# Routing of a two-layer diffusion block: unscaled router weights against modulated tokens, the norm's shift on VectorE, an earlier table load

## The chip, the cores and the metric

The kernel runs on one core of a Trainium2 chip. The metric is the device time of one execution in microseconds: the median of three runs of the kernel before is 1811.23 us (1810.03 to 1813.2).

## The reference

Two layers work on 256 latent tokens and 256 context tokens, each of width 1024. A layer normalises and modulates its tokens, mixes them (windowed attention with a sink beside a bidirectional gated recurrence), adds and normalises, and then sends them through 16 experts, each of which picks its own 32 tokens of a stream:

```python
mod = jax.nn.silu(c) @ w_mod[l] + b_mod[l]                 # 6 x 1024 columns, for both streams
u = layer_norm(x) * (1.0 + sc1) + sh1
y, yc = token_mixer(u, uc, w_in[l], ...)
x = post_norm(ALPHA * x + g1 * y, ln_g[l, 0], ln_b[l, 0])
u = layer_norm(x) * (1.0 + sc2) + sh2
x = post_norm(ALPHA * x + g2 * expert_choice_ffn(u, w_router[l], w_gate[l], w_up[l], w_down[l]), ...)

def expert_choice_ffn(u, w_router, w_gate, w_up, w_down):
    aff = softmax(u @ w_router)                            # (256, 16), float32
    top_w, top_idx = top_k(swapaxes(aff, 1, 2), 32)        # each expert picks 32 tokens
    h = silu(xs @ w_gate) * (xs @ w_up)                    # xs: the picked rows of u
    y = (h @ w_down) * top_w, added back to its tokens
```

In layer 0 both streams go through all of it; in layer 1 only the latent stream does.

## The kernel before, in words

Tokens stand in four tiles of 128 rows (`X[t]`), two for each stream; layer 1 has two. Everything is in one program whose instructions are put in a static order for each engine: a list scheduler takes the program's operations with their data dependences and with the tile buffers that they share, plays them against a model of durations, and writes down in which order each engine takes them. Some chains are fixed by `in_order`, and routing has a higher priority. At run time each engine takes its instructions strictly in that order, so an instruction that waits holds up all behind it. A DMA that GpSimd issues stands in GpSimd's order too.

The work runs through these stages. **Start** (to about 57 us): `crow` (the two conditioning vectors), the small parameter rows `rows` and the modulation biases `brow` are loaded into rotating 512-column buffers (`t2`, two of them), transposed by TensorE (L186, L205, L235/L236) and copied to columns. `mod_first` (L257 on) streams the modulation weights `wmod`, multiplies them by the conditioning columns `scol` in four groups (L267), turns the row by a transposition (L272) and adds the bias columns `bmod` (L276); the result `modT` is what every modulated token needs. ScalarE rounds the first input weights `win` to `wh` (L478), and VectorE and GpSimd each take half of the difference `wl` (L479); the projections (L168 to L170) are three matmuls for each product.

**Mixers**, then **post-norm**, then **routing** (`route`, one call for each stream): `ln_plain` normalises a token tile into `xh`. With `act` it is done on ScalarE as `r*x + (-mu*r)`; the column `mr` = -mu*r is made by two GpSimd multiplies (L343, L344), after the inverse root, which is a power on GpSimd (L333). TensorE transposes `xh` in two halves of 512 columns (L1061), which are copied to `u` (L1063, one by ScalarE and one by VectorE); the router weights, loaded to `wraw` (L1034) and scaled by the modulation on GpSimd (L1040), stand still and `u` moves past them in 128 columns (L1065). That leaves four partial sums on four bands of partitions; L1044/L1045 make the part of the shift, L1068 adds it, and L1070 folds the four bands and transposes to tokens x experts. Then softmax (L1072 to L1075, the exponential on ScalarE), the transposition to experts x tokens (L1077), four rounds of an eight-fold maximum (L1082/L1083), a scan that ranks the picked tokens (L1086 to L1088), and a one-hot matrix (L1102). **Experts**: the one-hot matrix gathers tokens by matmul (L1136), `modulate` writes them to `xs` (L383 on VectorE, L385 on ScalarE), and gate, up and down matmuls (L1218, L1251) run as their weights arrive. SyncE issues all weight loads in order; each waits until a buffer is free. At the very end `finish_out` (L1293 on) normalises the output, one half of a token tile on ScalarE and GpSimd, three on VectorE.

## Time and profile before

| | us |
|---|---|
| median of three runs | 1811.23 |
| profiled execution | 1812.94 |
| its span | 1811.2 |
| start, to the first steady projections | 0 to 57 |
| mixers of layer 0 | 57 to 500 |
| post-norm and routing of layer 0 | 500 to 535 |
| experts of layer 0 | 535 to 982 |
| mixers of layer 1 | 982 to 1325 |
| post-norm and routing of layer 1 | 1325 to 1356 |
| experts of layer 1, and the end | 1356 to 1811 |

TensorE is busy 1562.6 us (86%), VectorE 677.1 (37%), ScalarE 450.0 (25%), GpSimd 305.1 (17%); the DMA engines move 526 MB. By the page's chain of work that ended last, 53% of the span is TensorE's and 37% DMA's. How to read it: the shares are means over stages with different limits, so what an edit is worth is read in its own stage, from which wait ends last there. In a row of the timeline stand the start, the duration, the engine (PE is TensorE, DVE VectorE, ACT ScalarE, POOL GpSimd, SP SyncE), the line, the operation, the tile written and the tiles read, the shape, and in brackets how long the engine had been idle and what released it.

### The profile page before, as it was taken

What the parts mean: (1) busy time and instruction counts of PE and PEld (TensorE: products, weight loads), DVE (VectorE), ACT (ScalarE), POOL (GpSimd) and SP (SyncE); (2) the same over time, 40 slices, a digit from 0 to 9 for tenths busy, and PEclk for the clock granted to TensorE, in tenths of its full rate; (3) what the DMA queues carried; (4) which work ended last, traced back from release to release, by engine and by line L of the source; (5) the groups of instructions that cost most, each with busy time, mean ns of one, the idle gap of its engine ahead of it and who ended that gap; (6) DMA issues with size and microseconds to landing.
All of it is one profiled execution on the core that took longest, in us unless ns stands there. A gap on an engine that the chain in (4) does not pass through costs nothing.

```text
span 1811.2 us, 27388 instructions
## 1 busy us (share of the span) xinstructions
PE 1562.6 (86%) x11342; PEld 925.0 (51%) x11342; DVE 677.1 (37%) x1430; ACT 450.0 (25%) x850; POOL 305.1 (17%) x302
## 2 busy tenths in 40 slices
PE   6999999999989999997998899998968766666666
PEld 4777776688754433332323788775845222322222
DVE  4546566323661221211213756666751100100102
ACT  2436556323120100101000533576410000000000
POOL 2342121123310000000002633331610000000001
PEclk9999999999979999999999999999979777867887
DMA  9644123533679999999999653424689999999997
GB/s 323 186 117 127 60 82 129 177 126 117 245 308 385 421 421 421 421 422 421 421 421 379 208 178 105 130 92 131 241 341 408 421 421 422 420 421 421 421 421 287
DMA packets 159436, 526.06 MB, mean 290 GB/s; under 512 B 9896, under 2 KB 94064, under 8 KB 111184
## 3 DMA queue, kind: packets, MB, share of 16 engines
q1 hardware_dynamic: 157136, 517.46, 74.1%
q0 software_dynamic: 1456, 4.49, 0.7%
q10 hardware_dynamic: 720, 2.36, 0.4%
q8 instruction: 89, 1.46, 0.3%
q14 instruction: 35, 0.29, 0.0%
HBM read 523.23 MB, written 1.05 MB: 289 GB/s over the span
## 4 chain that ended last, share of the span: by engine, by line
PE 53%; DMA 37%; DVE 4%; ACT 2%; POOL 2%; issue 1%; SPq 1%; POOLq 0%; ACTq 0%; DVEq 0%
DMA w<-in_w_up_dram 13%; DMA w<-in_w_down_dram 12%; PE acc L168 9%; DMA w<-in_w_gate_dram 9%; PE acc L170 8%; PE acc L169 8%; PE acc L1218 8%; PE o L1251 4%; DMA wmod<-in_w_mod_dram 3%; PE md L294 2%; PE sc L701 2%; PE sc L724 1%; PE o L663 1%; PE tr L719 1%; PE hs L649 1%
## 5 line engine op out<-in xcount | busy, mean ns | idle before, releaser
L1218 PE MATMUL acc<-w,xs 128*32 128x256 f32 (+1 forms) x3064 | 402.9, 512 | 92.0 <-DMA w<-in_w_up_dram 48.9
L1218 PEld LDWEIGHTS acc<-w,xs 128*32 128x32 f32 (+1 forms) x3064 | 138.0, 130 | 339.2 <-issue 175.9
L1251 PE MATMUL o<-w,hT 128*32 128x256 f32 (+1 forms) x1432 | 188.9, 507 | 44.9 <-DMA w<-in_w_down_dram 30.5
L168 PE MATMUL acc<-uTh,wh 128*128 128x512 f32 (+1 forms) x592 | 215.1, 365 | 3.0 <-ACT qr L682 1.3
L169 PE MATMUL acc<-uTl,wh 128*128 128x512 f32 (+1 forms) x592 | 212.0, 358 | 1.4 <-DVE uTl L398 1.4
L170 PE MATMUL acc<-uTh,wl 128*128 128x512 f32 (+1 forms) x592 | 210.1, 355 | 0.0
L1229 ACT ACTIVATE h<-acc 128x512 f32<-128x512 f32 (+1 forms) x32 | 15.7, 491 | 522.2 <-PE acc L1218 509.4
L479 POOL TENSOR_TENSOR wl<-win,wh 128x1024 fp32r<-128x1024 f32 x44 | 113.4, 2579 | 164.3 <-ACT wh L478 164.3
L1251 PEld LDWEIGHTS o<-w,hT 128*32 128x32 f32 (+1 forms) x1432 | 63.5, 130 | 149.0 <-issue 66.7
L1230 DVE TENSOR_TENSOR h<-h,acc 128x512 f32<-128x512 f32 (+1 forms) x32 | 17.7, 552 | 293.4 <-PE acc L1218 293.4
L168 PEld LDWEIGHTS acc<-uTh,wh 128*128 128x128 f32 x592 | 111.9, 190 | 28.0 <-issue 6.7
L169 PEld LDWEIGHTS acc<-uTl,wh 128*128 128x128 f32 x592 | 112.3, 190 | 18.3 <-issue 2.8
L170 PEld LDWEIGHTS acc<-uTh,wl 128*128 128x128 f32 x592 | 112.1, 189 | 17.6 <-issue 3.4
L478 ACT CAST wh<-win 128x1024 fp32r<-128x1024 f32 x84 | 84.0, 1047 | 88.0 <-PE acc L169 61.9
L1110 POOL TENSOR_TENSOR OW<-OH,aff 128x256 f32<-128x256 f32 x8 | 4.9, 616 | 583.9 <-PE sc L1233 569.0
L1274 DVE TENSOR_TENSOR Y<-o,g2 OH 32x512 f32<-32x512 f32 x60 | 41.2, 687 | 140.1 <-PE o L1251 139.3
L479 DVE TENSOR_TENSOR wl<-win,wh 128x1024 fp32r<-128x1024 f32 x40 | 51.7, 1294 | 84.8 <-ACT wh L478 84.6
L1235 ACT COPY hT<-sc 128x512 f32<-128x512 f32 (+1 forms) x32 | 15.3, 479 | 243.1 <-PE sc L1233 243.1
L1274 DVE TENSOR_TENSOR Y g<-o,Y g 32x256 f32<-32x256 f32 x60 | 25.2, 420 | 122.0 <-PE o L1251 121.3
L294 PE MATMUL md<-wmod,scol 128*32 128x256 f32 x640 | 59.0, 416 | 7.8 <-DMA wmod<-in_w_mod_dram 5.6
L564 DVE TENSOR_TENSOR K<-K,F 128x512 f32<-128x512 f32 x56 | 46.6, 832 | 8.9 <-PE hs L630 5.4
L333 POOL TENSOR_TENSOR mv<-mv,nhalf 128x1 f32<-128x1 f32 x26 | 24.4, 942 | 126.7 <-DVE mv L332 126.0
(450 smaller groups left out, 2373.3 us busy)
## 6 DMA issues: line engine op xcount, KB each, us to landing
w<-in_w_gate_dram SPq DMA_DIRECT2D x128, 1024.0 KB, 19.8
w<-in_w_up_dram SPq DMA_DIRECT2D x127, 1024.0 KB, 19.8
w<-in_w_down_dram SPq DMA_DIRECT2D x119, 1024.0 KB, 19.8
wmod<-in_w_mod_dram SPq DMA_DIRECT2D x80, 512.0 KB, 4.6
win<-in_w_in_dram SPq DMA_DIRECT2D x26, 1024.0 KB, 5.4
win<-in_w_in_dram SPq DMA_DIRECT2D x32, 512.0 KB, 5.3
wmod<-in_w_mod_dram SPq DMA_DIRECT2D x32, 256.0 KB, 5.9
wo<-in_w_out_dram SPq DMA_DIRECT2D x8, 1024.0 KB, 5.0
```

Of the source, the lines that this page charges most:

```text
L168: mm(p, a.hi, b.hi, start=start, stop=False, **kw)
L169: mm(p, a.hi, b.lo, start=False, stop=False, **kw)
L170: mm(p, a.lo, b.hi, start=False, stop=stop, **kw)
L294: mm(pm[32 * j:32 * j + 32, 0:256], scol[:, k, :], w[:, 256 * j:256 * j + 256], start=(k == 0), stop=(k == KT - 1))
L333: pows.append(nc.gpsimd.tensor_tensor(mv[:, 2:3], mv[:, 2:3], nhalf[:, 0:1], op=ALU.pow))
L478: nc.scalar.copy(hi[:, r], w[:, r])
L479: ins = eng.tensor_sub(lo[:, r], w[:, r], hi[:, r])
L564: nc.vector.tensor_tensor(kv, kv, _view(f, 0, [[nf + 1, 2], [2, nf // 2], [0, m]]), op=ALU.mult)
L701: mm(p[:, :nk], qT[:, hd // 2, tk], kT[:, 2 * g + par, k0:k0 + nk], start=True, stop=True)
L1218: ins = mm(p[MW * j:MW * j + MW, :NW], xs[:, k, e4, :], wrow(w, k)[:, NW * j:NW * j + NW], start=(k == 0), stop=(k == KT - 1))
L1251: mm(py[MW * dj:MW * dj + MW, :NW], hT[:, 128 * m + MW * j:128 * m + MW * j + MW], wrow(wd, kt)[:, NW * dj:NW * dj + NW], start=(kt == 0), ...
L1274: nc.vector.tensor_tensor(o, py[r:r + 32, :NW], g2[r:r + 32, NW * dj:NW * dj + NW], op=ALU.mult)
```

## The change

- `wrt`, a permanent tile, takes the router weights unscaled. `router_load` issues its two loads of 32 KB on GpSimd's queue, for layer 0 among the mixers' first steps in the program text and for layer 1 after layer 0's first gather. The scaling, the memory fill, the bias matmuls, the shift's copy and the folding matmul go.
- In `route` the transposed tokens are modulated by scale and shift in four pieces of 128x128 for each half; for the last stream ScalarE and VectorE take the pieces in turn, before that ScalarE takes all. A piece stands still and 16 columns of router weights move past it; eight such matmuls for a token tile add up in PSUM, in a fixed order.
- `mr` is made by one VectorE instruction in `ln_plain` and in `finish_out`.
- `warm`, an exponential of one column, stands after the branches of the mixers.
- `sg` and `lt`, so far permanent tiles, come from the rotating pair `t2`.
- Two constant blocks of the table `cst` go.

```diff
-C_ID, C_ROT, C_COS, C_SIN, C_WM, C_TRI, C_ONE, C_IOTA, C_SEL, C_SUM, C_END = (
-    0, 128, 256, 512, 768, 1024, 1152, 1280, 1312, 1408, 1424)
+C_ID, C_ROT, C_COS, C_SIN, C_WM, C_IOTA, C_SEL, C_SUM, C_END = (
+    0, 128, 256, 512, 768, 1024, 1056, 1152, 1168)
...
+    wrt = P.tile([128, KT, NE], F32, name="wrt")
+
+    def router_load(l):
+        for i in range(2):
+            nc.gpsimd.dma_start(wrt[:, i::2], _dram(w_router, l * D * NE + i * NE, [[2 * NE, 128], [256 * NE, KT // 2], [1, NE]]))
...
-    sg = P.tile([128, 16], F32, name="sg")
+    sg = t2("sg")[:, :16]
...
-    lt = P.tile([128, 4, 2, HH], F32, name="lt")
+    lt = t2("lt")[:, :32].rearrange("p (a d h) -> p a d h", a=4, d=2)
...
-            nc.gpsimd.tensor_tensor(m, mu, r, op=ALU.mult)
-            pows.append(nc.gpsimd.tensor_tensor(m, m, neg, op=ALU.mult))
+            nc.vector.tensor_scalar(m, mu, -1.0, r, op0=ALU.mult, op1=ALU.mult)
...
             chains()
+            router_load(l)
...
+        warm = T.tile([128, 1], F32, name="warm", tag="warm", bufs=1)
+        nc.scalar.activation(warm, sgs[1, KT - 1][:, 0:1], AF.Exp)
...
-        wr = M["oT"].rearrange("p s (k e) -> p s k e", k=KT)
-        wraw = t2("wraw")[:, :KT * 32].rearrange("p (k e) -> p k e", e=32)
-        nc.gpsimd.memset(wraw, 0.0)
-        for i in range(2):
-            nc.gpsimd.dma_start(wraw[:, i::2, 0:NE], _dram(w_router, l * D * NE + i * NE, [[2 * NE, 128], [256 * NE, KT // 2], [1, NE]]))
-
-        pl = tr()
-        bcol = T.tile([128, 2], F32, name="bcol", tag="bcol")
-        for s in range(S):
-            for h in range(2):
-                nc.gpsimd.tensor_tensor(wr[:, s, 4 * h:4 * h + 4], wraw[:, 4 * h:4 * h + 4],
-                                        MT[l][:, 8 + h, :, s, None].to_broadcast([128, 4, 32]), op=ALU.mult)
-            for k in range(KT):
-                j = k % 4
-                mm(pl[32 * j:32 * j + 32, s:s + 1], wraw[:, k], MT[l][:, 6 + k // 4, j, s:s + 1], start=(k == j), stop=(k > j))
-        nc.vector.tensor_copy(bcol[:, 0:S], pl[:, 0:S])
...
+            busy = s == S - 1
+            turns = []
...
+                o = pl[:, NE * i:NE * i + NE]
                 for h in range(2):
...
-                    (nc.vector.tensor_copy if h else nc.scalar.copy)(u, p)
                     for m in range(4):
-                        mm(pl[32 * m:32 * m + 32, 128 * i:128 * i + 128], wr[:, s, 4 * h + m], u[:, 128 * m:128 * m + 128],
-                           start=(h == 0), stop=(h == 1))
-                lT = tp("lT")[:, :128]
-                nc.vector.tensor_scalar(lT, pl[:, 128 * i:128 * i + 128], bcol[:, s:s + 1], None, op0=ALU.add)
-                o = pl[:, 256 + NE * i:256 + NE * i + NE]
-                mm(o, lT, cst[:, C_SUM:C_SUM + NE], start=True, stop=True)
+                        um, k = slice(128 * m, 128 * m + 128), 4 * h + m
+                        modulate(busy and m % 2, u[:, um], p[:, um], l, 3, 4, k, s)
+                        in_order(turns, mm(o, u[:, um], wrt[:, k], start=(k == 0), stop=(k == KT - 1), skip_group_check=True))
...
+        if not last:
+            router_load(l + 1)
...
-            nc.gpsimd.tensor_tensor(m, *sc[0], op=ALU.mult)
-            nc.gpsimd.tensor_tensor(m, m, neg, op=ALU.mult)
             seq = []
+            in_order(seq, nc.vector.tensor_scalar(m, sc[0][0], -1.0, sc[0][1], op0=ALU.mult, op1=ALU.mult))
```

The static order changes with it, also where the text does not. GpSimd at the start, before (`brow` the modulation biases, `wl` the difference halves of the first input weights):

```order
L198 DMA msk<-in_msk_dram 128x192
L200 DMA sink<-in_attn_sink_dram 128x16
L203 DMA rows<-in_hgrn_lb_fw_dram 8x128
L203 DMA rows<-in_hgrn_lb_bw_dram 8x128
L203 DMA rows<-in_hgrn_norm_g_dram 8x128
L333 ISA
L333 TENSOR_TENSOR mv<-mv,nhalf 128x1
L232 DMA brow<-in_b_mod_dram 48x256
L333 TENSOR_TENSOR mv<-mv,nhalf 128x1 x3
L479 TENSOR_TENSOR wl<-win,wh 128x1024 x2
```

The same engine and place after the change, in the new file's line numbers (L235 is the load of `brow`, L481 the difference, L186 the router weights):

```order
L201 DMA msk<-in_msk_dram 128x192
L203 DMA sink<-in_attn_sink_dram 128x16
L186 DMA wrt<-in_w_router_dram 128x4x16 x2
L336 ISA
L336 TENSOR_TENSOR mv<-mv,nhalf 128x1
L206 DMA rows<-in_hgrn_lb_fw_dram 8x128
L206 DMA rows<-in_hgrn_lb_bw_dram 8x128
L206 DMA rows<-in_hgrn_norm_g_dram 8x128
L336 TENSOR_TENSOR mv<-mv,nhalf 128x1 x3
L481 TENSOR_TENSOR wl<-win,wh 128x1024 x2
L235 DMA brow<-in_b_mod_dram 48x256
```

The load of `brow` has moved behind three powers and two differences, the loads of `rows` behind the first power, and the router loads stand ahead of it all.

TensorE at the start, before, from the transpositions of `brow` on (`xh` normalised tokens, `md` the modulation row, `uTh`/`uTl` modulated tokens; a count is of issued instructions, where the trace counts two for each of these float32 matmuls):

```order
L235 MATMUL o<-cst,brow 128x48
L236 MATMUL o<-cst,brow 128x48
L235 MATMUL o<-cst,brow 128x48
L236 MATMUL o<-cst,brow 128x48
L272 MATMUL md<-cst,row 128x128
L376 MATMUL o<-cst,xh_149 128x128 x4
L376 MATMUL sc<-cst,xh_149 128x128 x8
L267 MATMUL md<-wmod,scol 32x128 x16
L168 MATMUL acc<-uTh,wh 128x512 x2
```

The same engine and place after (L238/L239 the transpositions of `brow`, L270 the modulation matmuls, L378 the tokens' transpositions, L166 to L168 the projections):

```order
L208 MATMUL o<-cst,rows 128x24
L275 MATMUL md<-cst,row 128x128
L238 MATMUL o<-cst,brow 128x48
L239 MATMUL o<-cst,brow 128x48
L238 MATMUL o<-cst,brow 128x48
L239 MATMUL o<-cst,brow 128x48
L378 MATMUL o<-cst,xh_148 128x128 x4
L270 MATMUL md<-wmod,scol 32x128 x32
L378 MATMUL sc<-cst,xh_148 128x128 x4
L166 MATMUL acc<-uTh,wh 128x512
L167 MATMUL acc<-uTl,wh 128x512
```

Behind `brow` now stand all 32 modulation matmuls of the second group ahead of the first projection, where 16 stood before.

VectorE in layer 1's routing, after, from the normalisation of the second token tile's post-norm to the logits (`X_3197` that token tile, `u_10108` and the like the modulated pieces, `r_10131` the first maximum of the softmax):

```order
L372 SCALAR_TENSOR_TENSOR X_3197<-X_3197,mv,lnp 128x1024
L326 BN_STATS st<-X_3197 128x6
L385 TENSOR_SCALAR u_10108<-sc,modT_108 128x128
L326 BN_STATS st<-X_3197 128x6
L385 TENSOR_SCALAR u_10122<-sc,modT_108 128x128
L385 TENSOR_SCALAR u_10108<-sc,modT_108 128x128
L332 BN_AGGR mv<-st 128x2
L335 TENSOR_SCALAR mv<-mv 128x1
L385 TENSOR_SCALAR u_10122<-sc,modT_108 128x128
L349 TENSOR_SCALAR xh<-X_3197,mv 128x1024
L1062 TENSOR_REDUCE r_10131<-tr 128x1
```

Before, the two statistics stood side by side there, and one copy of 128x512 stood between the statistics and the normalisation of the second token tile; now four pieces stand among them.

## Rows read from the trace of the kernel before

**Rows 1.** By stage, layer 0: us, busy by engine, clock, DMA share, GB/s.

```profile
57.00:500.00 443.00, 436.00 (x2925) 324.28 (x2924) 234.21 (x495) 197.33 (x376) 129.09 (x110) 0.99 0.41 136
...
500.00:535.00 35.00, 27.66 (x242) 20.77 (x242) 27.29 (x87) 9.27 (x21) 4.50 (x9) 0.71 0.78 323
```

**Rows 2.** GpSimd's timeline at the start: start, duration, instruction, idle before.

```profile
6.80 0.60 POOL L232 DMA_DIRECT2D brow<-in_b_mod_dram  x1
...
26.66 2.44 POOL L479 TENSOR_TENSOR wl<-win,wh 128x1024 fp32r<-128x1024 f32 x1 [1.17 <-ACT wh L478]
```

**Rows 3.** Landing of the DMAs of the tile brow.

```profile
DMA to landing us min/median/max: 6.1/6.1/6.1
```

**Rows 4.** Landing of the DMAs of the tile rows.

```profile
DMA to landing us min/median/max: 7.4/7.5/7.5
```

**Rows 5.** Two stretches of the start, columns as in group 1.

```profile
6.00:8.00 2.00, 0.25 (x1) 0.17 (x1) 2.00 (x5) 0.56 (x2) 1.13 (x2) 1.00 1.14 197
...
28.00:30.00 2.00, 2.00 (x16) 1.11 (x8) 2.00 (x2) 0.00 (x0) 1.10 (x1) 0.69 1.10 355
```

**Rows 6.** TensorE's timeline at the start.

```profile
18.06 0.26 PE L235 MATMUL o<-cst,brow 48*128 48x48 f32 x1
...
25.96 2.67 PE L267 MATMUL md<-wmod,scol 128*32 128x128 f32 x32
...
39.60 0.71 PE L168 MATMUL acc<-uTh,wh 128*128 128x512 f32 x2
...
45.38 1.95 PE L267 MATMUL md<-wmod,scol 128*32 128x128 f32 x64
...
47.27 0.66 PE L376 MATMUL sc<-cst,xh 128*128 128x128 f32 x4
...
47.68 0.70 PE L168 MATMUL acc<-uTh,wh 128*128 128x512 f32 x2
```

**Rows 7.** VectorE's timeline at the start.

```profile
19.65 0.23 DVE L276 TENSOR_TENSOR modT<-md,bmod 128x4 f32<-128x4 f32 x2
...
25.67 1.23 DVE L479 TENSOR_TENSOR wl<-win,wh 128x1024 fp32r<-128x1024 f32 x1 [1.20 <-ACT wh L478]
```

**Rows 8.** Two stretches ahead of expert weights, columns as in group 1.

```profile
530.00:535.00 5.00, 4.39 (x35) 4.04 (x36) 2.07 (x6) 2.00 (x5) 0.00 (x0) 1.00 0.00 0
...
1354.00:1356.00 2.00, 2.00 (x22) 1.88 (x24) 0.82 (x2) 0.92 (x2) 0.00 (x0) 1.00 0.00 0
```

**Rows 9.** VectorE in layer 0's routing.

```profile
515.03 0.69 DVE L1063 COPY u<-sc 128x512 f32<-128x512 f32 x1 [0.87 <-PE sc L1061]
...
517.40 0.35 DVE L1068 TENSOR_SCALAR lT<-hs,bcol 128x128 f32<-128x128 f32 x1
...
529.42 0.41 DVE L383 TENSOR_SCALAR xs<-o,modT 128x128 f32<-128x128 f32 x1 [0.53 <-ACT xs L385]
```

**Rows 10.** TensorE in layer 0's routing.

```profile
517.81 0.61 PE L1070 MATMUL hs<-cst,lT 128*128 128x16 f32 x2 [0.16 <-DVE lT L1068]
```

**Rows 11.** GpSimd in layer 1's routing.

```profile
1328.66 1.90 POOL L333 TENSOR_TENSOR mv<-mv,nhalf 128x1 f32<-128x1 f32 x2 [4.63 <-DVE mv L332]
...
1330.81 1.13 POOL L344 TENSOR_TENSOR mr<-mr,neg 128x1 f32<-128x1 f32 x1
```

**Rows 12.** ScalarE in layer 1's routing.

```profile
1331.97 1.24 ACT L345 ACTIVATE xh<-X,mr,mv 128x1024 f32<-128x1024 f32 x1 [23.84 <-POOL mr L344]
...
1338.63 1.28 ACT L1073 ACT_TABLE_LOAD   x1
```

**Rows 13.** GpSimd at the front of layer 1.

```profile
1000.66 0.28 POOL L344 TENSOR_TENSOR mr<-mr,neg 128x1 f32<-128x1 f32 x1
```

**Rows 14.** GpSimd at the end.

```profile
1802.02 0.55 POOL L333 TENSOR_TENSOR mv<-mv,nhalf 128x1 f32<-128x1 f32 x1 [65.03 <-DVE mv L332]
...
1806.25 1.59 POOL L1307 TENSOR_TENSOR X<-X,lnp 128x512 f32<-128x512 f32 x1
```

**Rows 15.** ScalarE at the end.

```profile
1804.05 0.78 ACT L1305 ACTIVATE X<-hs,mr,mv 128x512 f32<-128x512 f32 x1 [16.41 <-POOL mr L1298]
```

More of the change, by code (lines that the diff above doesn't have):

```diff
@@ L68, in _shape_tables @@
     cst[:, C_WM + 128:C_WM + 256] = np.where(j >= p, 0.0, NEG)
-    cst[:, C_TRI:C_TRI + 128] = (p < j)
-    cst[:, C_ONE:C_ONE + 128] = 1.0
     cst[:, C_IOTA:C_IOTA + 32] = np.arange(1, 33)[None, :]
@@ L182, in tile_kernel @@
     nc.gpsimd.memset(nhalf, -0.5)
-    neg = P.tile([128, 1], F32, name="neg")
-    nc.gpsimd.memset(neg, -1.0)
+    wrt = P.tile([128, KT, NE], F32, name="wrt")
+    def router_load(l):
+        for i in range(2):
+            nc.gpsimd.dma_start(wrt[:, i::2], _dram(w_router, l * D * NE + i * NE, [[2 * NE, 128], [256 * NE, KT // 2], [1, NE]]))
     pt = tr()
```

## The prediction

> **What bounds the kernel now.** I read the views in this order: the stage table, the start's timelines, the DMA landings, the rows around the two routings, the tail. In the stage table the reader sees that layer 0's mixers are TensorE's: 436.0 of 443 us busy, DMA at 0.41, and in the routing stage behind them it is still 27.66 of 35 [rows 1]. Behind routing the kernel waits for expert weights, but these cannot run ahead: just before the first gate matmuls the DMA share is 0.00 in layer 0 and again in layer 1 [rows 8], because the weight buffers are full until the experts start. So whatever is gained or lost ahead of a first expert matmul, at the start of the kernel too, goes on to the end. That makes the first 57 us, where TensorE waits for modulation, as important as the two routings.
>
> **The start: the bias load moves behind GpSimd's casts.** Before, GpSimd issues the DMA of `brow` (all modulation biases) at 6.80, and it lands 6.1 us later, long before TensorE transposes it at 18.06 [rows 2, 3, 6]. The change takes `sg` and `lt` out of the permanent pool into the two rotating buffers of `crow`, `rows` and `brow`; a static order is planned with that, and in it the issue of `brow` stands behind both weight subtractions of GpSimd, the second of which starts at 26.66 and takes 2.44 [rows 2]. These wait for ScalarE's casts, and those for the first weights, none of which the change makes earlier. So the issue comes at 26.66 + 2.44 = 29.10.
>
> Landing: the row for this very DMA is 6.1, and for the three small ones of `rows` it is 7.4 to 7.5 [rows 3, 4]. Both ran while the DMA engines were full (share 1.14 in 6 to 8), and at 28 to 30 the share is 1.10 [rows 5], so I take 6.1: the transposes begin at 35.2 and not at 18.06. The ends are 0 us (then 29.7, the issue alone) and 7.5 (36.6). The two router loads of 32 KB that now ride in the full stream at the very beginning I book at nothing; their cost, if any, lies inside that upper end. VectorE's two subtractions also stand ahead of its small work now, but the later one ends at 25.67 + 1.23 = 26.90 [rows 7], with eight microseconds to spare.
>
> The Trainium skill gives another price here ("DMA: Bandwidth & Descriptors", section "Anatomy of one DMA — SWDGE (gpsimd) path"): about 2.0 us fixed plus the bytes over 436 GB/s, an estimate of 2.1 for 48 KB. The transposes would then begin at 31.2. The trace does not agree in a full stretch: 6.1 and 7.4 [rows 3, 4], and the measurement decides.
>
> Behind the waiting transposes, on TensorE's own queue, stand the modulation matmuls of the second group and every projection matmul, so the engine stands still. From the start of the transposes to the end of the first modulation columns it took 19.65 + 0.23 - 18.06 = 1.82 [rows 6, 7]; that gives 37.0. Then come 64 modulation matmuls, which cost 1.95 at the full clock and 2 x 2.67 = 5.34 at the rate seen after TensorE's pause before 25.96, where the stage's clock was low [rows 6]. After an even longer pause I take 4.4: 41.4. Four transposes (0.66) bring the first projection to 42.1. One group's period before was 47.68 - 39.60 = 8.08; in the new order each carries four transposes more, so about 8.7. Two periods: 59.5 for the point that stood at 47.68. By then TensorE has done the same matmuls in both kernels. **Delay: 59.5 - 47.68 = 11.8 us.** With a landing of 3 us it is 8.7; at the outer ends (at once, full clock; 7.5, half clock) 3.9 and 14.1. The mixers behind keep their order on TensorE and VectorE, and TensorE has 7.0 us idle in 443 there, each bit waiting for work that moves along [rows 1]. So nothing takes the delay in.
>
> **Routing, layer 0: +1.0.** Away goes, for the last token tile, the copy with the bias (0.35) and the folding matmul (0.61) [rows 9, 10]: -0.96. One copy of 128x512 (0.69) becomes four modulations of 128x128, alternating between ScalarE and VectorE on one PSUM bank. How that runs is to be seen at `xs`, the same kind of alternation: each VectorE piece waits 0.53 for ScalarE's [rows 9]. So the two engines don't overlap on one bank, and four hand-overs cost 4 x 0.53 - 0.69 = +1.43. In the gather the two banks change places in ScalarE's order, and the first gate matmul waits one hand-over more: +0.53. Sum +1.0. Ends: -1.0 if the pieces overlap, +2.5 if the second half pays as well. Router scaling and the bias matmuls leave GpSimd and TensorE; they lie beside the post-norm, so I book nothing. The exponential's table load moves among the mixers, where ScalarE is busy 197 of 443 [rows 1]: nothing either.
>
> **Front of layer 1: -0.3.** One of two GpSimd multiplies ahead of the normalisation goes (0.28) [rows 13]. Ends -1.5 and +0.5.
>
> **Routing, layer 1: -1.3.** The normalisation starts at 1331.97, right behind the negation (1330.81 + 1.13), which stood behind two powers (1328.66, 1.90) [rows 11, 12]. With the shift on VectorE behind the first power (half of 1.90, so 1329.6) it could start 2.1 earlier. But that is the first token tile; the second is normalised by VectorE, which now has quarter copies and a wait for GpSimd ahead of it. I count 0.5 of the 2.1. The table load of 1.28 at 1338.63 lies between two logit copies and the exponential, on the path: -1.28 [rows 12]. Links -0.96 and quarters +1.43 as in layer 0. Sum -1.3; ends -4.3 (everything counts, no price for the quarters) and 0.
>
> **Tail: -0.8.** The power ends at 1802.57, but ScalarE's half starts only at 1804.05, behind a second power and the negation; GpSimd's last add, at 1806.25 for 1.59, follows from it [rows 14, 15]. At most 1.25 is to be had; VectorE, which now waits for that power too, gives some back. Ends -1.25 and 0.
>
> **Sum.** 11.8 + 1.0 - 0.3 - 1.3 - 0.8 = +10.4 on the profiled execution's 1812.94 (span 1811.2). That execution is 1.7 above the median of 1811.23, so I put the difference on the median: **1821.6**.
>
> **Rivals.**
> - *The biases land quickly*, in about 3 us. For it: 48 KB is little. Against it: all four rows of that queue in a full stretch. Delay 8.7, time 1818.5. The page's price named above would mean 7.8 and 1817.6.
> - *The last stream's routing becomes the longer one.* VectorE now waits for GpSimd's power and takes pieces in turn with ScalarE, and its reductions queue behind those pieces; both routings at their upper ends are +2.8 more: 1824.5. For it: the 0.53 waits. Against it: the pieces for the first tokens lie beside other work.
> - *The routing gains in full*: the first tile's 2.1 us carries through, and the quarters cost nothing: layer 0 at -1.0, layer 1 at -4.3, so 11.8 - 1.0 - 0.3 - 4.3 - 0.8 = +5.4, 1816.6.
> - *Not slower: the late start is swallowed.* Place: between the first projections and layer 0's first gate matmul. If something other than TensorE set the end of the mixers, a start up to 11.8 us late would cost nothing, and the rest gives 1.0 - 0.3 - 1.3 - 0.8 = -1.4: 1809.8. It decides from the point where TensorE has more than about 8 us to spare in layer 0's mixers; it has 7.0, in pieces that themselves hang on its own chain [rows 1]. For it speaks only that matmul ends are modelled, so a busy engine may hide slack.
>
> **How the numbers follow.** A difference under 0.2% (3.6 us) can't be told from none here. Chances: forecast 0.66 (its own range 1818 to 1825.5), quick landing 0.14, longer routing 0.07, full gain 0.05, swallowed 0.08. The first four are slower, but for some 0.04 where short landing and good routing meet: slower 0.87. Same holds that and half of the swallowed case, 0.08; faster 0.05. The range reaches down to 1813, past the full gain with a quick landing, and up to 1826, which takes in the 14.1 us delay.
>
> **What would show it.** Right: the issue of `brow` near 29.1, TensorE idle from about 20 to near 35, the point at 47.68 near 59.5, and the same distance at the last projection of layer 0 (some 12 us) and at the first gate matmul (some 13). In layer 1's routing no table load, `xh` about two microseconds earlier against the stage's beginning, the first expert matmul about one. Wrong: TensorE at its projections before 36; a distance that shrinks inside the mixers; or pieces of ScalarE and VectorE that overlap on one bank, which would take the +1.43 out of both routings.

## The result and the profile after

The changed kernel takes 1822.82 us (median of 4 runs, 1819.99 to 1824.11), the kernel before 1811.55 in the same session: a ratio of 1.0062, 95% interval 1.0047 to 1.0077, so 8.5 to 14 us slower. The forecast was 1821.6. The profiled execution took 1822.02 us, its span is 1820.2 (before 1812.94 and 1811.2).

**The start.** GpSimd's timeline of the changed kernel (start, duration, instruction, idle before and what ended it), which answers to [rows 2]:

```profile
26.81 2.47 POOL L481 TENSOR_TENSOR wl<-win,wh 128x1024 fp32r<-128x1024 f32 x1 [0.81 <-ACT wh L480]
29.23 0.60 POOL L235 DMA_DIRECT2D brow<-in_b_mod_dram  x1
```

The issue of `brow` stands behind the second weight subtraction and comes at 29.23, not at 6.80. Its landing, from the view of the tile, answers to [rows 3]:

```profile
DMA to landing us min/median/max: 5.4/5.4/5.4
```

TensorE's timeline of the changed kernel answers to [rows 6]:

```profile
32.83 0.45 PE L275 MATMUL md<-cst,row 128*128 128x128 f32 x1 [13.67 <-DVE row L273]
34.70 0.34 PE L238 MATMUL o<-cst,brow 48*128 48x48 f32 x1 [1.43 <-DMA brow<-in_b_mod_dram]
...
37.14 3.64 PE L270 MATMUL md<-wmod,scol 128*32 128x128 f32 x64
...
41.46 0.48 PE L166 MATMUL acc<-uTh,wh 128*128 128x512 f32 x1
...
58.52 0.71 PE L166 MATMUL acc<-uTh,wh 128*128 128x512 f32 x2
```

TensorE stands idle for 13.67 us, does one matmul, and waits for `brow` again. The point that stood at 47.68 is at 58.52: +10.84. The first of the two waits was not in the prediction. It ended on VectorE, whose timeline at the start answers to [rows 7]:

```profile
27.21 2.09 DVE L217 TENSOR_TENSOR lt<-cols 128x8 f32<-128x8 f32 x1
...
32.40 0.28 DVE L273 COPY row<-md 128x128 f32<-128x128 f32 x1
...
36.09 0.23 DVE L279 TENSOR_TENSOR modT<-md,bmod 128x4 f32<-128x4 f32 x2
```

The lower bounds (`lt`) had moved behind the subtractions too, and the copy that TensorE needed stood behind them. That chain let TensorE go 1.9 us before `brow` did (32.83 and 34.70), so `brow` set the end.

**From there on.** The stage row of layer 0's mixers, with the columns of [rows 1], shows TensorE as full as before (436.51 of 443, before 436.00), so the delay has nowhere to go:

```profile
57.00:500.00 443.00, 436.51 (x2978) 324.23 (x2971) 231.27 (x497) 202.30 (x383) 127.29 (x106) 0.99 0.40 128
```

This table follows it; each time is read off a timeline of the two traces (us, the same instruction in both):

| point | before | after | later by | in this stage |
|---|---|---|---|---|
| third group's first projections | 47.68 | 58.52 | 10.84 | start +10.8 |
| last softmax maximum of layer 0's routing | 518.60 | 529.69 | 11.09 | mixers and logits +0.25 |
| first gate matmul | 534.60 | 543.74 | 9.14 | ranks and gather -1.95 |
| last matmul of layer 0's experts | 988.21 | 998.32 | 10.11 | +1.0 |
| first normalised half for layer 1 | 1000.97 | 1012.21 | 11.24 | front +1.1 |
| last projection of layer 1 | 1324.64 | 1334.27 | 9.63 | -1.6 |
| one-hot of layer 1 | 1350.19 | 1359.19 | 9.00 | -0.6 |
| first expert matmul of layer 1 | 1355.93 | 1366.37 | 10.44 | gather +1.4 |
| last matmul | 1800.52 | 1809.62 | 9.10 | -1.3 |
| last output DMA | 1807.87 | 1816.73 | 8.86 | tail -0.2 |

The start is the whole loss; no other row moves it by more than 2.0 us. These are one execution of each kernel, and the executions of the kernel before in all sessions lay between 1806.4 and 1817.8, so a row of +1 or -1.6 in stages that the change doesn't touch is no finding. The first of the two routing rows holds all of the mixers as well: layer 0's last projection is at 500.37 before and at 512.14 after, 11.77 later, so from there to the last maximum the changed kernel gains 0.7 us.

**Layer 0's routing.** TensorE in the kernel before, at its end:

```profile
527.79 2.05 PE L1136 MATMUL acc<-OH,xh 128*128 128x128 f32 x16
529.77 0.29 PE L1091 MATMUL hs<-cst,wk 16*128 16x16 f32 x2
```

and in the changed kernel:

```profile
530.79 0.38 PE L1067 MATMUL o<-cst,aff 128*16 128x128 f32 x1 [0.16 <-DVE aff L1065]
531.14 3.78 PE L1126 MATMUL acc<-OH,xh 128*128 128x128 f32 x16
534.72 2.79 PE L1126 MATMUL o<-OH,xh 128*128 128x128 f32 x16
...
538.00 0.29 PE L1081 MATMUL hs<-cst,wk 16*128 16x16 f32 x2
...
543.74 4.51 PE L1210 MATMUL acc<-w,xs 128*64 128x512 f32 x20 [0.55 <-ACT xs L387]
```

Before, stream 1's ranks `wk` were ready at 527.41 (the last product, 527.00 for 0.41 on VectorE), but their transposition stood on TensorE behind stream 0's gather until 529.77: 2.4 us in the queue. After, `wk` is ready at 537.40 and transposed at 538.00. That is 1.8 which the prediction does not have, and 1.1 more lies between the maximum and `wk`: before, stream 0's ranks still stood between stream 1's on VectorE. The two prices that it does have are there: 0.55 at the gate for ScalarE's piece of `xs`, and the hand-overs between the engines on one bank. The last four pieces start at 525.11 (ScalarE), 525.66 (VectorE), 526.09 (ScalarE) and 526.83 (VectorE), one behind the other, and take 2.10 us together where 4 x 0.53 = 2.12 was forecast. One of VectorE's waits for ScalarE's piece:

```profile
520.53 0.41 DVE L385 TENSOR_SCALAR u<-sc,modT 128x128 f32<-128x128 f32 x1 [0.47 <-ACT u L387]
```

**Layer 1's routing.** ScalarE starts the normalisation at 1337.88 [rows 12], 5.9 later than before where the stage began 9.6 later: 3.7 earlier against it (2.1 had been expected), and there is no table load in the stage.

```profile
1337.88 1.24 ACT L347 ACTIVATE xh<-X,mr,mv 128x1024 f32<-128x1024 f32 x1 [19.99 <-DVE mr L346]
```

VectorE's tile is 1.2 earlier against the stage's beginning (0.5 had been counted), the one-hot 0.6. From that tile's normalisation to the last maximum the changed kernel takes 7.24 us and the kernel before 6.65. The last of the tile's pieces ends 5.41 us after the normalisation's begin, where the copies ended after 3.63; the two links that are gone give 1.2 back behind it. And the table load was not all on the path. Before, it ended at 1338.63 + 1.28 = 1339.91, and the maximum that the exponential needs as well ended at 1339.61, so it alone held the exponential for 0.3 us:

```profile
1339.44 0.17 DVE L1072 TENSOR_REDUCE r<-tr 128x1 f32<-128x16 f32 x1
```

Then the gather loses the rest, and more. The changed kernel's stretches there (columns as in [rows 1]; the clock stands after the five busy times):

```profile
1361.00:1363.00 2.00, 2.00 (x11) 2.00 (x11) 0.00 (x0) 0.00 (x0) 0.00 (x0) 0.50 0.00 0
1363.00:1365.00 2.00, 2.00 (x12) 2.00 (x11) 0.49 (x2) 0.92 (x2) 0.00 (x0) 0.50 0.00 0
1365.00:1367.00 2.00, 2.00 (x21) 1.67 (x24) 0.36 (x2) 0.46 (x1) 0.00 (x0) 0.80 0.00 0
```

In the kernel before, the stretch that holds the second half of the gather is at 1.00 [rows 8]. Both kernels have TensorE idle for 5.77 us ahead of the ranks' transposition, after which the clock is at 0.50, the lower of its two levels. Here it came back later, and the two halves took 3.78 and 3.19 instead of 3.45 and 2.05. The second half takes 2.54, 2.59 and 2.67 in e7b_shift_only, e7_shift_table and e7c_table_only below, behind an idle time of 5.77 to 5.78 as well, so in one execution of each it lies anywhere between the two.

**The tail.** ScalarE's half starts at 1811.95, 2.3 after the last matmul at 1809.62 (before 3.5), and GpSimd's last add ends 0.8 sooner against that matmul. But the last output is no longer theirs. VectorE's last half ends 7.08 behind the last matmul (before 6.19), and its DMA is issued behind it:

```profile
1811.95 0.78 ACT L1296 ACTIVATE X<-hs,mr,mv 128x512 f32<-128x512 f32 x1 [12.84 <-DVE mr L1290]
...
1815.73 0.97 DVE L1301 SCALAR_TENSOR_TENSOR X<-X,mv,lnp 128x512 f32<-128x512 f32 x1
1816.73 0.33 SPq L1302 DMA_DIRECT2D out_dram<-X  x1
```

In the kernel before, where the last output followed GpSimd's add [rows 14]:

```profile
1805.66 1.05 DVE L1310 SCALAR_TENSOR_TENSOR X<-X,mv,lnp 128x512 f32<-128x512 f32 x1
```

So the output's issue comes 0.24 us sooner against the last matmul, 7.11 instead of 7.35.

### The profile page after: what moved, and what is told of

It reads as the page before. It is cut to its first block, busy times and chain, and to the rows that moved or that the text cites. A ratio compares the mean times of both kernels' runs of the same rounds, so it can differ in the third digit from the quotient of the medians.

```text
span 1820.2 us, 27267 instructions
## 1 busy us (share of the span) xinstructions
PE 1579.4 (87%) x11282; PEld 939.3 (52%) x11282; DVE 680.4 (37%) x1440; ACT 459.9 (25%) x878; POOL 299.5 (16%) x277
## 5 line engine op out<-in xcount | busy, mean ns | idle before, releaser
L1210 PE MATMUL acc<-w,xs 128*32 128x256 f32 (+1 forms) x3064 | 412.6, 524 | 86.6 <-DMA w<-in_w_up_dram 49.8
L1243 PE MATMUL o<-w,hT 128*32 128x256 f32 (+1 forms) x1432 | 194.1, 525 | 40.5 <-DMA w<-in_w_down_dram 26.0
L166 PE MATMUL acc<-uTh,wh 128*128 128x512 f32 (+1 forms) x592 | 215.4, 365 | 1.7 <-ACT sgs L842 0.9
L168 PE MATMUL acc<-uTh,wl 128*128 128x512 f32 (+1 forms) x592 | 209.9, 355 | 0.0
L481 POOL TENSOR_TENSOR wl<-win,wh 128x1024 fp32r<-128x1024 f32 x44 | 114.6, 2605 | 162.1 <-ACT wh L480 162.0
L166 PEld LDWEIGHTS acc<-uTh,wh 128*128 128x128 f32 x592 | 111.7, 189 | 26.4 <-issue 6.3
L168 PEld LDWEIGHTS acc<-uTh,wl 128*128 128x128 f32 x592 | 111.9, 189 | 17.8 <-issue 3.4
L481 DVE TENSOR_TENSOR wl<-win,wh 128x1024 fp32r<-128x1024 f32 x40 | 52.3, 1308 | 87.4 <-ACT wh L480 87.2
```

Of the source, the lines that this page charges most:

```text
L166: mm(p, a.hi, b.hi, start=start, stop=False, **kw)
L168: mm(p, a.lo, b.hi, start=False, stop=stop, **kw)
L481: ins = eng.tensor_sub(lo[:, r], w[:, r], hi[:, r])
L1210: ins = mm(p[MW * j:MW * j + MW, :NW], xs[:, k, e4, :], wrow(w, k)[:, NW * j:NW * j + NW], start=(k == 0), stop=(k == KT - 1))
L1243: mm(py[MW * dj:MW * dj + MW, :NW], hT[:, 128 * m + MW * j:128 * m + MW * j + MW], wrow(wd, kt)[:, NW * dj:NW * dj + NW], start=(kt == 0), ...
```

## Experiments

Theory: the rotating buffers put `brow` behind the subtractions, and this start is the loss; the rest comes to about nothing. Rivals: the loss is in the new routing, or it is another effect of the moved loads. Each ratio is to runs of the kernel before on the same chip, with its 95% interval.

**e2_rotating: the start alone.** The kernel before with nothing but this:

```diff
-    sg = P.tile([128, 16], F32, name="sg")
+    sg = t2("sg")[:, :16]
-    lt = P.tile([128, 4, 2, HH], F32, name="lt")
+    lt = t2("lt")[:, :32].rearrange("p (a d h) -> p a d h", a=4, d=2)
```

> The kernel before with nothing changed but sg and lt in the rotating pair. Theory A: bias load issued near 29, time 1811.5 + 10.8 = about 1822. Rival B: 1811.5, as before.

Measured: 1822.36 us, 1.0059 (1.0047 to 1.0071). Two lines that compute nothing make the whole loss of the changed kernel. Its start, GpSimd and TensorE:

```profile
28.74 0.60 POOL L232 DMA_DIRECT2D brow<-in_b_mod_dram  x1
```

```profile
34.22 0.34 PE L235 MATMUL o<-cst,brow 48*128 48x48 f32 x1 [1.44 <-DMA brow<-in_b_mod_dram]
...
57.25 0.70 PE L168 MATMUL acc<-uTh,wh 128*128 128x512 f32 x2
```

**e1_permanent: the changed kernel with both lines undone.**

> The changed kernel with sg and lt back in permanent tiles; the static order then issues the bias load right behind GpSimd's first power. Theory A (the late bias load is the loss): issue near 9 us, first projections near 28.5, and the time falls by the 10.8 us that the second group's projections stood later in the trace (47.68 to 58.52), to about 1812; routing, shift and table load together then weigh about +0.5 to -2 against the kernel before. Rival B (the late start is taken in by the mixers, the loss is in routing): the time stays at 1822.

Measured: 1819.1 us, 1.0037 (1.0025 to 1.0049). `brow` is issued at 6.83 and the loss is still 6.7 us, where the theory had about none. The start has a second trap. VectorE in this kernel:

```profile
23.59 0.57 DVE L243 COPY bmod<-o 128x24 f32<-128x24 f32 x6
24.08 1.84 DVE L246 TENSOR_SCALAR bmod<-bmod 128x16 f32<-128x16 f32 x1
25.88 1.23 DVE L481 TENSOR_TENSOR wl<-win,wh 128x1024 fp32r<-128x1024 f32 x1
27.02 2.31 DVE L246 TENSOR_SCALAR bmod<-bmod 128x16 f32<-128x16 f32 x1
29.25 0.22 DVE L279 TENSOR_TENSOR modT<-md,bmod 128x4 f32<-128x4 f32 x2
```

The biases are transposed by 22.19, but their copies stand behind VectorE's first subtraction (from 22.45) in the planned order, and the small operation L246 takes 1.84 and 2.31 us where the changed kernel's two together take 0.24. GpSimd in the same stretch:

```profile
23.44 2.44 POOL L481 TENSOR_TENSOR wl<-win,wh 128x1024 fp32r<-128x1024 f32 x1 [7.81 <-ACT wh L480]
26.87 2.43 POOL L481 TENSOR_TENSOR wl<-win,wh 128x1024 fp32r<-128x1024 f32 x1 [0.99 <-ACT wh L480]
```

Both of VectorE's operations end within 0.04 us of GpSimd's (25.92 and 25.88, 29.33 and 29.30): they began behind it and ended with it. `modT` comes at 29.25 instead of 19.65, and the third group's projections at 52.73, 5.0 late. In this one trace little of that is left at layer 0's first gate matmul (535.14 for 534.60) and the loss stands again at layer 1's last projection (1329.89 for 1324.64). So that the trap is the whole of the 6.7 us isn't shown by the trace. The times speak for it: f9_turn_first below, which takes the trap away and fixes the place of one transposition, is 7 us under this kernel.

**e1b_lt_rotating: only `sg` undone.**

> The changed kernel with sg permanent and lt still rotating: the bias load stands behind all four powers of the start, but ahead of the two subtractions; issue near 16.5, landing near 22 to 22.6. Theory A says that the delay follows the landing: TensorE's transposition of the biases at 22 and not 18, so 2 to 5 us over e1, about 1815. Rival C (it is the place behind the subtractions, not the landing as such, that costs, since ScalarE and VectorE stand behind casts and subtractions too there): within 1 us of e1.

Measured: 1821.62 us, 1.0053 (1.0041 to 1.0065); the expectation missed. `brow` is issued at 16.86 and transposed at 23.23, but the copies stand behind the subtraction here too, `modT` comes at 29.67, and about 3 us more are gone by layer 0's last projection (6.56 late), in mixers that were planned anew.

**e8_routing_only: the kernel before with the new routing and loads, but neither buffers nor shift nor table.**

> The kernel before with the new routing alone (unscaled weights loaded early, quarter modulations, 16 moving columns); sg and lt permanent, the shift on GpSimd, no early table load. By the prediction's terms: layer 0 +1.0, layer 1 without the table load and the shift +0.5 to +1, so 1813. By what the trace after shows (layer 0's first gate matmul 1.7 us earlier than the late start alone would give, layer 1's gather 1.4 us longer at the low clock): 1810 to 1812.

Measured: 1814.57 us, 1.0019 (1.0010 to 1.0029), above both expectations (1813, and 1810 to 1812), with `modT` at 29.12 and the third group's projections at 51.87, 4.2 late. So the copies' place comes with the router loads on GpSimd, not with the buffers.

**f5_start_restored: the changed kernel with permanent buffers and layer 0's router loads ordered behind GpSimd's second subtraction.** e8b_routing_start_restored is e8_routing_only with the same order.

```diff
+            if l == 0:
+                in_order(rgate, ins)
```

> The changed kernel with sg and lt permanent and the two router loads of layer 0 chained behind GpSimd's second subtraction of the start. In the static order VectorE's copies of the biases then stand ahead of its first subtraction again, as in the kernel before; the order of the mixers is that of the changed kernel. Theory A2 (the start's loss has two causes, both by order: the rotating buffers put the bias load late, and the router loads on GpSimd push VectorE's bias copies behind the subtractions, which is why e1 got only a part back): third group's first projections near 47.7, time 1822.8 - 10.8 = 1812, 7 below e1. Rival B2 (e1's remaining loss is in the routing itself): 1818 to 1819.

> The kernel before with the new routing alone, and the router loads chained behind GpSimd's second subtraction. Theory A2: the 4.2 us that the third group's projections stood late in e8 go, so 1814.6 - 4.2 = 1810.4. Rival B2: 1814 to 1815, as e8.

Measured: 1815.99 us, 1.0024 (1.0014 to 1.0035), and 1815.9 us, 1.0027 (1.0016 to 1.0038). The start is as before (48.03 and 47.44 for 47.68), and 4 to 5 us stay lost; 1812 and 1810.4 had been expected. TensorE in f5_start_restored:

```profile
522.45 3.78 PE L1133 MATMUL acc<-OH,xh 128*128 128x128 f32 x16 [0.51 <-DVE OH L1099]
526.02 0.42 PE L1074 MATMUL o<-cst,aff 128*16 128x128 f32 x1
526.81 2.82 PE L1133 MATMUL o<-OH,xh 128*128 128x128 f32 x16 [0.37 <-DVE wk L1075]
...
533.82 0.27 PE L1088 MATMUL hs<-cst,wk 16*128 16x16 f32 x2 [2.63 <-DVE wk L1085]
534.69 3.37 PE L1133 MATMUL o<-OH,xh 128*128 128x128 f32 x16 [0.60 <-DVE mk L1102]
537.86 2.37 PE L1133 MATMUL acc<-OH,xh 128*128 128x128 f32 x16
```

With another start the planner put stream 1's last softmax transposition (526.02) behind half of stream 0's gather. The ranks start late, TensorE runs dry for 2.63 us, and the second gather takes 3.37 and 2.37. In the changed kernel that transposition stood ahead of the gather.

**f6_by_bank: f5_start_restored with ScalarE and VectorE each on a whole bank in the last stream.**

```diff
-                        modulate(busy and m % 2, u[:, um], p[:, um], l, 3, 4, k, s)
+                        modulate(busy and h, u[:, um], p[:, um], l, 3, 4, k, s)
```

> As f5, but for the last stream ScalarE takes all four pieces of the first half and VectorE all four of the second, so that each engine has a PSUM bank to itself. Theory C (the two engines don't overlap on one bank, so the turns cost the hand-overs): the pieces of the two halves overlap, layer 1's logits come 0.7 to 1.5 earlier, time 1 below f5. Rival D (TensorE's eight small matmuls in their fixed order, or VectorE's queue, bind): within 0.5 of f5, or above it.

Measured: 1811.28 us, 0.9996 (0.9985 to 1.0007), 4.7 under f5_start_restored where 1 was expected. It looked like a large price for sharing a bank, but the planner had also put the transposition ahead of the gather by itself. One run more had to part the two.

**f9_turn_first: f5_start_restored with the transposition ordered ahead of the gather, the pieces alternating.**

```diff
-                nc.tensor.transpose(pt[:NE, :128], aff[:, i, :], ident)
+                turned[:] = [nc.tensor.transpose(pt[:NE, :128], aff[:, i, :], ident)]
...
-            gather(0, s)
+            gather(0, s, turned)
```

> The kernel f5_start_restored with one thing added: TensorE does the last softmax transposition of stream 1 before it begins stream 0's first gather. In f5_start_restored's profile the transposition stood behind eight matmuls of that gather, VectorE waited 3.66 us for it, the rank of stream 1 came 1.2 us later than the reduce before it, and TensorE then stood idle for 2.63 us and did the second gather at a lower clock (first gate matmul 5.56 us later than before's). In f6_by_bank, which changed which engine evicts which piece, the planner had put the transposition ahead of the gather by itself, so that kernel can't tell the two apart. Theory, TensorE's order costs most of it: about 4 of f5_start_restored's 4.7 us over f6_by_bank come back, 1812 us, one-hot of stream 1 at about +2.2 instead of +4.0, first gate matmul at about +2.2 instead of +5.6. Rival, two engines taking turns on one PSUM bank cost it: 1815.5 us, the first gate matmul stays at +5. Between the two: both share it, 1813.5 us.

Measured: 1812.06 us, 0.9998 (0.9987 to 1.0010): level with f6_by_bank. TensorE:

```profile
521.66 0.38 PE L1074 MATMUL o<-cst,aff 128*16 128x128 f32 x1 [0.94 <-DVE aff L1072]
521.84 3.62 PE L1133 MATMUL acc<-OH,xh 128*128 128x128 f32 x16
525.25 2.75 PE L1133 MATMUL o<-OH,xh 128*128 128x128 f32 x16
...
528.50 0.29 PE L1088 MATMUL hs<-cst,wk 16*128 16x16 f32 x2
...
529.76 2.15 PE L1133 MATMUL acc<-OH,xh 128*128 128x128 f32 x16 [0.21 <-DVE OH L1099]
531.75 2.05 PE L1133 MATMUL o<-OH,xh 128*128 128x128 f32 x16
...
534.35 7.95 PE L1217 MATMUL acc<-w,xs 128*64 128x512 f32 x36 [0.55 <-ACT xs L391]
```

TensorE doesn't run dry, the second gather takes 2.15 and 2.05, and the first gate matmul is 0.25 earlier than before's instead of 5.56 later. So the order cost it; taking turns on a bank, against a bank each, makes no difference beyond the 2 us or so that the intervals leave. Turns do cost in the pieces themselves: the second token tile's eight pieces of layer 1 take 2.7 us here and 2.2 in f6_by_bank, but the last maximum stands 17.00 and 16.92 us behind the last projection, because TensorE's small matmuls end about 2 us after the last piece in both. The two kernels' orders also differ elsewhere in layer 0.

**e7_shift_table, e7b_shift_only, e7c_table_only: the kernel before with the two small edits, old routing and old start.** The shift is the change's L346 and L1290 (one VectorE operation for two of GpSimd), the table its early exponential.

> The kernel before with the shift on VectorE and the early table load alone, old routing, start order unchanged in its main rows. By the prediction's terms: tail -0.8, front -0.3, layer 1's routing -0.5 for the first tile's normalisation and -1.3 for the table load: -2.9, so 1808.6. If VectorE's waits for the power eat it: 1811.5.

> The kernel before with norm's shift on VectorE alone (layer norms of the fronts and the tail), without the early exponential table: it splits the gain of 2.9 us of e7_shift_table. Theory: shift brings 0.8 us at the tail and 0.3 to 1 at the fronts, and the table the rest, about 1.3 at layer 1: 1809.6 us. Rival: the gain is the planner's different order of the mixers, which the shift alone makes too (the table adds one instruction): 1808.2 us. Second rival: the order comes with the table's instruction, and the shift brings its tail alone: 1810.3 us.

> The kernel before with the early exponential (the table sooner) alone. e7_shift_table (shift and table) gained 2.9 us and e7b_shift_only 6.3 us, so the table's part is +3.4 us if the two add up. Theory of the prediction: at layer 1 a table load of 1.28 us leaves the path of the third and fourth token tile's norm, and one of the same length is put among the weight casts of the last mixer, where ScalarE has room: -1 us, 1810 us. Rival, the two add up and the early table costs: 1814.5 us, one-hot of stream 1 or the first gate matmul of layer 0 late by 2 us or more. Second rival, it does nothing that can be measured: within 0.7 us of before, and the 3.4 us between e7_shift_table and e7b_shift_only are the scatter of the rounds.

Measured: both 1806.86 us, 0.9984 (0.9974 to 0.9994), the sum that was expected (-2.9), though not its terms; the shift alone 1805.02 us, 0.9963 (0.9951 to 0.9975), more than any theory had; the table alone 1812.5 us, 1.0006 (0.9994 to 1.0018). The shift alone is the fastest version found, 6.7 us under the kernel before. Its trace accounts for little of that in the stages that the shift touches: layer 0 from the last projection to the first gate matmul -1.5 (32.70 for 34.23), layer 1's same stretch -1.0 (30.31 for 31.29), tail -0.2 (7.11 for 7.35), and against them the front of layer 1 +1.7 (14.47 for 12.76, from layer 0's last expert matmul to ScalarE's half). 4.0 more lie in layer 0's mixers, whose order on TensorE is the same. They arise between 326 and 345 us, where the profiled execution of the kernel before had the lower clock and this one the full clock:

```profile
330.00:334.00 4.00, 3.59 (x18) 1.64 (x18) 0.00 (x0) 0.37 (x1) 0.00 (x0) 0.50 0.64 200
```

```profile
330.00:334.00 4.00, 3.79 (x31) 1.76 (x32) 0.98 (x2) 1.58 (x4) 0.66 (x1) 1.00 0.76 241
```

The table alone is ahead there by much the same (3.1 us at the point that stands at 343.7 before) in its profiled execution, and none in its median. So where the shift's 6.7 us come from is open.

The table alone shortens that stretch of layer 1 by 1.1 (30.21), but not all of that is the table load. The second tile's transpositions ran at a granted clock of 1.00 in its execution, and eight of them took 1.19 us; in the kernel before and in the two kernels with the shift the clock was 0.50 there, and before's eight took 1.95.

The kernel with both and the one with the shift alone, at the same clock there, differ by the table load: 30.06 and 30.31, so 0.25 us, near the 0.3 that was on the path. In the ratios the table's part is undecided: 1.1 us slower alone (-1.1 to +3.3), 3.8 slower on top of the shift.

**f11_turn_first_no_table: f9_turn_first without the early exponential.**

> The kernel f9_turn_first (the changed kernel with its start restored and the last softmax transposition ahead of the first gather) without the early exponential: 1812.1 us with it. Theory, the early table helps at layer 1: 1 us slower without, 1813. Rival, it costs as between e7_shift_table and e7b_shift_only: 1808.7 us. If neither, 1812.

Measured: 1812.48 us, 1.0010 (1.0001 to 1.0020), for 0.9998 with it. This leans to the table helping by some 2 us in the new routing, against the two comparisons above, but the intervals overlap.

## Why the prediction was right, step by step

**Start, +11.8 forecast, +10.84 in the trace: right, and shown.** e2_rotating has this step alone and gives the whole loss. The step lies 1.0 under its size. The issue was forecast at 29.10 and came at 29.23; the landing took 5.4, not 6.1; the 64 matmuls after the pause 3.64, not 4.4; the first projection came at 41.46, not 42.1. The Trainium skill ("DMA: Bandwidth & Descriptors", section "Anatomy of one DMA — SWDGE (gpsimd) path") would give about 2.1 for this DMA as an estimate; the 5.4 here does not agree.

What the step missed was a second chain: `lt` and the copy of `row` freed TensorE only at 32.83. Had `brow` landed in 2.1 us, at 31.3, the start would have hung on VectorE. And the sentence that VectorE had eight microseconds to spare took its small operations at their short durations; beside GpSimd's subtraction one took 2.09.

**"Nothing takes the delay in": right.** Layer 0's last projection is 11.77 late, where some 12 was forecast, behind 440 us of mixers.

**Router loads at nothing: wrong as a rule, harmless here.** e1_permanent and e8_routing_only show their price, 5.0 and 4.2 us at the start, through the order that they cause. In the changed kernel `brow` is later than that and hides it.

**Routing, layer 0, +1.0 forecast, -1.7 in the trace: a step that failed.** The hand-overs have their forecast size, 2.10 for 2.12, and so has the one at the gate, 0.55 for 0.53; pieces that overlap, the forecast's sign of being wrong, were not seen there. At the first gate matmul, where some 13 us were forecast, 9.14 are left. What was left out is the work of stream 0 ahead of stream 1's last steps: TensorE's gather, worth 1.8 in the changed kernel's favour, and VectorE's ranks, worth 1.1. f5_start_restored and f9_turn_first show how much that place decides: one transposition on the other side of the gather is 4 us.

**Front, -0.3 forecast, +1.1 in the trace: wrong in its sign.** The forecast took a GpSimd multiply off the path and kept all else. But those multiplies also stood between the power and GpSimd's next subtraction of 128x1024. In the kernel before, VectorE's half of the normalisation runs ahead of that subtraction, which starts at 1000.89:

```profile
1000.34 0.55 DVE L339 TENSOR_SCALAR hgT<-X,mv 128x512 f32<-128x512 f32 x1 [2.05 <-POOL mv L333]
```

In the changed kernel the subtraction starts at 1009.37, 0.06 us ahead of it, and the half takes 2.56:

```profile
1009.43 2.56 DVE L342 TENSOR_SCALAR hgT<-X,mv 128x512 f32<-128x512 f32 x1 [1.01 <-POOL mv L336]
```

`mr`, now VectorE's, waits behind it. e7b_shift_only has this edit alone, and shows the same:

```profile
993.88 4.85 POOL L476 TENSOR_TENSOR wl<-win,wh 128x1024 fp32r<-128x1024 f32 x2
993.94 2.57 DVE L337 TENSOR_SCALAR hgT<-X,mv 128x512 f32<-128x512 f32 x1 [0.99 <-POOL mv L331]
```

The half takes 2.56 or 2.57 in all nine kernels with the shift, and 0.54 or 0.55 in the five without it. So at this place the shift's edit costs time.

**Routing, layer 1, -1.3 forecast, +0.8 in the trace: wrong in its sign.** Of the shift more came through than was counted, 1.2 for 0.5, but the table load, booked at -1.28, was on the path for 0.3 only, and the pieces took back what was left: the one-hot gained 0.6 where 1.3 was booked. The gather then gave back 1.4 at the lower clock, which the forecast didn't consider. In e7b_shift_only, e7_shift_table and e7c_table_only the gather is 0.8 to 0.9 longer than in the kernel before, too, and takes back part of what they gain ahead of it (1.8 to 2.1 at the one-hot).

**Tail, -0.8 forecast, -0.24 in the trace: the mechanism right, its size not.** ScalarE's half and GpSimd's add are sooner as forecast, but VectorE's last half, which "gives some back", now ends last and gives back nearly all. The two kernels with the shift have the same -0.24.

**The sum.** Behind the start -1.4 was forecast. In the trace the four stages that had a term come to about nothing (-1.7 + 1.1 + 0.8 - 0.2), and those without one to about -2 (+1.0, -1.6 and -1.3), which is no finding by one execution of each. Layer 0's routing came out 2.7 better than forecast, the start 1.0 better, layer 1's routing 2.1 worse, the front 1.4 and the tail 0.6. So the mechanism of the loss was right, but that the total lies within 1.2 us of the forecast is luck in part: the errors cancel, and the two profiled executions differ by 9.1 us where the medians differ by 11.3. f9_turn_first, which holds all of the change but its start, with TensorE in the changed kernel's order around the gather, measures -0.4 (-2.4 to +1.8). The rivals fall with e2_rotating: the delay isn't swallowed, and no routing makes the loss.

## What to carry to other kernels

Where a planner sets the order, a tile's pool is an ordering edit: ask which DMA issues and copies may now be planned behind a wait, on every queue, before asking what the new arithmetic costs. When one variant is 4 us off another, compare their order at the last dependent step ahead of the stage's end before pricing the edited instructions; a bank assignment that seemed to gain 4.7 us had gained nothing that the runs can tell from the order's part. An operation taken off an engine lets the next one on it start sooner: ask whom that one stands beside. And test the small edits alone: here the kernel with one of them is 6.7 us faster, for a reason that is still open, and in the change it can't be seen.

## What the runs showed of the hardware

VectorE's small operations were stretched beside GpSimd's subtractions of 128x1024: 2.09 us for 128x8 (0.17 for the next one like it), 1.84 and 2.31 for 128x16, each ending within 0.04 us of GpSimd's; and 2.56 for 128x512 (0.55 otherwise), which ended 0.28 behind it. The Trainium skill has this ("SBUF — State Buffer", section "Who interferes with whom"): a pair of ports that VectorE shares with GpSimd is an exclusive lock, and of two instructions that need it the one issued second blocks until the first is done. The trace agrees: GpSimd's subtraction from 26.81 ends at 29.28, VectorE's `lt`, which began at 27.21, at 29.30.

With TensorE idle for the same 5.77 us ahead of layer 1's gather, the granted clock in the gather's second half was 1.00 in the kernel before, and 0.50 and then 0.80 in the changed one. The gather's halves together are 1.47 us longer there; what makes the difference wasn't tested, and it is one execution of each.

A spell of the lower clock inside the mixers, where TensorE's order is the same, went with about 3 to 4 us between the profiled execution of the kernel before and those of e7b_shift_only and e7c_table_only.
